# A hybrid decoder trunk: half of the conv norm's rounding copies by ScalarE, the second half of the output weights asked for later, and another figure for GpSimd's additions in the scheduler's table

## Chip, cores and metric

One core of a Trainium2 chip. The metric is the device time of one execution in microseconds; lower is better. The engines are TensorE (PE), VectorE (DVE), ScalarE (ACT), GpSimd (POOL) and SyncE (SP), which here issues all the transfers.

## What is computed

x is 1024 tokens by 1024 channels, float32. Layer 1 mixes tokens by a causal convolution, layer 2 by sliding-window attention; after each come a norm, a squared-ReLU MLP with a norm, and a gated per-layer embedding. The change is about the first mixer and the norm and product behind it:

```python
def conformer_conv(x, w_in, b_in, w_dw, b_dw, ln_g, ln_b, w_out, b_out):
    h = x @ w_in + b_in
    a, gate = jnp.split(h, 2, axis=-1)
    h = a * jax.nn.sigmoid(gate)
    h = lax.conv_general_dilated(
        h, w_dw[:, None, :], window_strides=(1,), padding=[(CONV_WIDTH - 1, 0)],
        dimension_numbers=("NWC", "WIO", "NWC"), feature_group_count=D_MODEL) + b_dw
    h = jax.nn.silu(layer_norm(h, ln_g, ln_b))
    return h @ w_out + b_out
...
    for i in range(DEPTH):
        y = conformer_conv(...) if i < N_A_LAYERS else swa_sink_attention(...)
        x = layer_norm(DEEPNORM_ALPHA * x + y, mix_ln_g[i], mix_ln_b[i])
        x = layer_norm(DEEPNORM_ALPHA * x + sq_relu_mlp(x, mlp_w_up[i], mlp_w_down[i]), mlp_ln_g[i], mlp_ln_b[i])
        x = x + (p[i] @ ple_w_proj[i]) * jax.nn.sigmoid(x @ ple_w_gate[i])
```

DEPTH is 2, D_MODEL 1024, CONV_WIDTH 31, and N_A_LAYERS 1.

## The kernel before

**Products in three parts.** TensorE works in a rounded float32 (fp32r). To keep float32's accuracy each operand is split into a rounded high part and the rest, xh and xl, wh and wl, and each product is three: xh with wh, xh with wl, xl with wh. A split is a rounding copy (xh from x) and a subtraction (xl = x - xh). The copy of a weight is ScalarE's, its subtraction VectorE's; a weight comes as raw from a DMA, in units of 128 x 1024.

**The scheduler.** The program is not issued as it is written. A Recorder notes every operation, schedule() (line 334) then orders them, and issue() emits them from line 485, which is why all rows of the trace have L485. schedule() is a list scheduler: it plays the program through with a duration for each operation from cost() (line 304), takes the operation that can start first and among those the one written first (later(by) adds to that rank, after(x) makes an operation depend on x in the plan), and hands out buffers by tag from a fixed number of slots (SLOTS: five t, four z, two raw, five wh and wl, four E and so on). The plan fixes each engine's order and which buffer each tile gets; on the chip the engines follow that order and wait for real data. Operations of the engine "either" go to VectorE or GpSimd, whichever the plan has free first: an addition in the norm and one in the embedding. The plan also knows that VectorE and GpSimd share something: an operation on one that reads two operands from SBUF is lengthened by what the other still holds (lines 346 to 357, and `held`). So one changed duration can move operations on all engines from there on.

**The conv stage** (to about 250 us). For each of eight channel blocks c, TensorE makes a and gate from x (most by a seven-product scheme with sums t, g). VectorE and ScalarE gate them, split the result (zz) and hand it over through DRAM (scr), from where it comes back in another layout (B). The 31 taps are products with band matrices E, which ScalarE and VectorE build from the weights z: a rounding copy into the upper half and a subtraction into the lower half. One channel block (OWN) is done without TensorE: ScalarE multiplies (z from B), GpSimd adds (cst), VectorE does the other half (g). The result goes by transposes (tr) into Z, tiles of tags X and A.

**The conv norm and the output product** (from about 250 us). conv_ln(t0) takes two token tiles of 128, t0 = 0, 2, 4, 6: statistics, one scaling on VectorE (X) and one on GpSimd (A), then for f = 0, 2, 4, 6 four transposes, two silu activations by ScalarE into a tile t, and the split of t: the rounding copy xh (512 columns) and the subtraction xl, both VectorE's. The output product has two halves of columns; each half's weights are four units of two channel blocks, and token tiles 0 to 3 (t0 = 0 and 2) are taken before tiles 4 to 7. Units 0 and 1 of the first half are asked for ahead of the norm, units 2 and 3 (called 713 and 718 in the order, their split parts 750, 751 and 754, 755) after the first silu.

Of the kernel before, what the change touches and what calls it, by code (L numbers as in the profile page):

```python
# [13 lines left out]
ALU = mybir.AluOpType  # L14
# [198 lines left out]
class Recorder:  # L213
# [90 lines left out]
    def cost(self, o, outs, allv):  # L304
        e, n = o.eng, o.name
        f = outs[0].n if outs and isinstance(outs[0], View) else 1024
        if e == "tensor":
            if n == "transpose":
                return 113.5
            return max(109.0, f * 0.4427 + 5.5 * (f < HT))  # L310
        if e == "sync":
            return 380.0
        if e == "scalar":
            t = 60.0 + f * 0.85
            if n == "activation":
                t += sum(c for k, c in (("bias", 90.0), ("scale", 130.0), ("accum_out", 110.0)) if isinstance(o.kw.get(k), View))
            return t
        if e == "gpsimd":
            if n == "tensor_tensor":
                return 460.0 if o.kw["op"] == ALU.pow else 90.0 + 2.2 * f  # L320
            return 160.0 + 1.17 * f
        psum = any(v.buf.space == "PSUM" for v in allv)
        if n == "tensor_scalar" and not psum:
            return 100.0 + f * 0.69
        if n == "bn_stats":
            return 69.0 + 1.042 * allv[-1].n
        if n == "reduce_max":
            return 70.0 + allv[-1].n * 1.042
        if n == "reciprocal":
            return 60.0 + 6.3 * f  # L330
        t = 120.0 if isinstance(o.kw.get("scalar"), View) else 70.0
        return t + f * 1.042
# [185 lines left out]
class Emit:  # L518
# [353 lines left out]
    def conv(self):  # L872

        nc, d, ws = self.nc, self.d, self.ws
# [330 lines left out]
        def conv_ln(t0):  # L1205

            zs = []
            for t in (t0, t0 + 1):
                z = [Z[t // 4, t % 4, q] for q in range(2)]
                rs = self.stats(z)  # L1210
                for q in range(2):
                    (nc.gpsimd if q else nc.vector).tensor_scalar(out=z[q], in0=z[q], scalar1=rs[:, 0:1], scalar2=rs[:, 1:2], op0=ALU.mult, op1=ALU.add)
                zs.append(z)
            for f in range(0, KB, 2):
                blk = [slice((f + j) % 4 * P, ((f + j) % 4 + 1) * P) for j in range(2)]
                ps = self.transpose4([z[f // 4][:, b] for b in blk for z in zs], SLACK)
                sv = self.sb("t")
                for j in range(2):
                    half = slice(2 * j * P, 2 * (j + 1) * P)
                    nc.scalar.activation(  # L1220
                        sv[:, half], ps[:, half], AF.Silu, bias=lb[:, f + j : f + j + 1], scale=lg[:, f + j : f + j + 1]
                    )
                    silu.append(nc.ops[-1])
                sl = (slice(None), slice(f % 4, f % 4 + 2), slice(t0 % 4 * P, (t0 % 4 + 2) * P))
                sv = sv.rearrange("p (a b) -> p a b", a=2)
                xh, xl = (x[sl] for x in self.xT[f // 4, t0 // 4])
                nc.vector.tensor_copy(xh, sv)
                nc.vector.tensor_tensor(out=xl, in0=sv, in1=xh.bitcast(F32), op=ALU.subtract)

        second = [self.load_xT(1, kb) for kb in range(KB)]  # L1230
# [14 lines left out]
        ins = (x for c in range(8) for x in conv_in(c))  # L1245
        outs = (x for c in range(8) for x in taps(c))
        alone = taps_alone()
        made = 0
        for n in range(32 + LAG):
            next(ins, None)  # L1250
            if n >= LAG:
                next(outs, None)
            made += OWN_RATE if n >= OWN_FROM else 0
            while made >= 1:
                next(alone, None)
                made -= 1
            if n == 32:
                idle = (x[:, k, :] for q in (1, 0) for x in self.xT_quarter((q, 1), F32) for k in range(4))
                fill = self.embed(0, (0, 1), idle, lambda *v: stores.append(v))
            for k in range(WOVEN[n - 32] if n >= 32 else 0):  # L1260
                next(fill)
# [24 lines left out]
        marks, silu = [], []  # L1286
        for t in range(0, NT, 2):
            conv_ln(t)
            if t == 0:
                with nc.after(silu[0]):  # L1290
                    ws.add(*[d["w_out"][0, u] for u in range(2, 4)])
                    ws.pump()
            marks.append(self.xT[1, t // 4][1].buf.last)
# [955 lines left out]
```

## Time and profile before

| | us |
|---|---|
| median of 3 runs (lowest, highest) | 2121.67 (2120.52, 2124.4) |
| the profiled execution | 2122.42 |
| its span | 2120.7 |
| PE busy in it | 2101.1 (99%) |
| DVE busy | 1721.8 (81%) |
| ACT busy | 1233.0 (58%) |
| POOL busy | 323.8 (15%) |

The granted TensorE clock is 1.00 over the stretches that the prediction reads. A row of the timeline gives the start in the span, the duration, the engine, the line, the operation, output<-inputs by the names of the program, the count, and in brackets how long the engine was idle before and what ended that. A row of the groups gives the count, the busy time and the mean duration in ns, then the idle time ahead of it. Since matmuls overlap, their durations are longer than the time from one to the next.

### The profile page before, as it was taken

What the parts mean: (1) busy time and instruction counts of PE and PEld (TensorE: products, weight loads), DVE (VectorE), ACT (ScalarE), POOL (GpSimd) and SP (SyncE); (2) the same over time, 40 slices, a digit from 0 to 9 for tenths busy, and PEclk for the clock granted to TensorE, in tenths of its full rate; (3) what the DMA queues carried; (4) which work ended last, traced back from release to release, by engine and by line L of the source; (5) the groups of instructions that cost most, each with busy time, mean ns of one, the idle gap of its engine ahead of it and who ended that gap; (6) DMA issues with size and microseconds to landing.
All of it is one profiled execution on the core that took longest, in us unless ns stands there. A gap on an engine that the chain in (4) does not pass through costs nothing.

```text
span 2120.7 us, 29661 instructions
## 1 busy us (share of the span) xinstructions
PE 2101.1 (99%) x9912; PEld 1738.4 (82%) x9912; DVE 1721.8 (81%) x2754; ACT 1233.0 (58%) x2335; POOL 323.8 (15%) x551
## 2 busy tenths in 40 slices
PE   9999999999999999999999999999999999999999
PEld 7888888888888888888878878888888888888887
DVE  8899799987777879876975878699787768788688
ACT  6767644766566533334656888466666663333373
POOL 0523114100000000002131656150000000000041
PEclk9999999999999999999999999999999999999999
DMA  6668855887787747564586112677877885575735
GB/s 228 190 201 284 290 188 173 296 269 246 260 268 262 259 163 243 185 201 152 174 296 230 36 66 80 219 247 253 277 271 257 272 305 174 181 252 163 246 111 202
DMA packets 216601, 459.56 MB, mean 217 GB/s; under 512 B 21888, under 2 KB 52864, under 8 KB 216448
## 3 DMA queue, kind: packets, MB, share of 16 engines
q1 hardware_dynamic: 216448, 457.67, 64.3%
q8 instruction: 78, 1.28, 0.2%
q14 instruction: 75, 0.61, 0.1%
HBM read 311.57 MB, written 146.01 MB: 216 GB/s over the span
## 4 chain that ended last, share of the span: by engine, by line
PE 75%; ACT 3%; DVE 3%; DMA 2%; issue 1%; POOL 1%; SPq 0%; DVEq 0%; POOLq 0%; ACTq 0%
PE ps L485 57%; PE tr L485 18%; ACT z L485 2%; DVE z L485 1%; DVE t L485 1%; DMA wh<-gate_t 1%; DMA t<-proj 0%; POOL sm L485 0%; DVE sm L485 0%; ACT t L485 0%; DMA raw<-in_w_q_dram 0%; ACT wh L485 0%; DMA hid<-zz 0%; DVE g L485 0%; ACT g L485 0%
## 5 line engine op out<-in xcount | busy, mean ns | idle before, releaser
L485 PE MATMUL ps<-xh 128*128 128x512 f32 x636 | 247.4, 389 | 0.0
L485 PE MATMUL ps<-xl,xh 128*128 128x512 f32 x636 | 247.4, 389 | 0.0
L485 PE MATMUL ps<-xh,xl 128*128 128x512 f32 x636 | 247.4, 389 | 0.0
L485 POOL TENSOR_SCALAR sm<-sm 128x1 f32<-128x1 f32 x72 | 26.3, 369 | 1358.2 <-DVE A L485 624.7
L485 PE MATMUL ps<-xl,wh 128*128 128x512 f32 x484 | 189.4, 392 | 0.0
L485 PE MATMUL ps<-xh,wh 128*128 128x512 f32 x484 | 188.0, 392 | 1.0 <-ACT t L485 0.8
L485 PE MATMUL ps<-xh,wl 128*128 128x512 f32 x484 | 188.7, 390 | 0.0
L485 ACT CAST wh<-raw 128x1024 fp32r<-128x1024 f32 (+2 forms) x134 | 119.4, 895 | 87.0 <-PE ps L485 58.8
L485 PE MATMUL ps<-wh,xh 128*128 128x512 f32 x412 | 162.8, 396 | 3.0 <-DMA wh<-gate_t 2.0
L485 PE MATMUL ps<-wh,xl 128*128 128x512 f32 x412 | 162.7, 396 | 0.0
L485 PE MATMUL ps<-wl,xh 128*128 128x512 f32 x412 | 162.4, 395 | 0.0
L485 ACT CAST xh<-wh 128x1024 fp32r<-128x1024 f32 x76 | 79.7, 1049 | 118.6 <-PE ps L485 82.2
L485 PEld LDWEIGHTS ps<-xl,xh 128*128 128x128 f32 x636 | 119.4, 188 | 24.9
L485 PEld LDWEIGHTS ps<-xh,xl 128*128 128x128 f32 x636 | 119.3, 188 | 24.8
L485 PEld LDWEIGHTS ps<-xh 128*128 128x128 f32 x636 | 119.4, 188 | 24.7
L485 DVE TENSOR_TENSOR wl<-raw,wh 128x1024 fp32r<-128x1024 f32 (+2 forms) x100 | 98.5, 986 | 46.8 <-ACT wh L485 46.7
L485 ACT CAST wh<-g 128x512 fp32r<-128x512 f32 x136 | 80.9, 619 | 86.5 <-PE ps L485 48.5
L485 DVE TENSOR_TENSOR wl<-g,wh 128x512 fp32r<-128x512 f32 x136 | 92.0, 701 | 36.6 <-ACT wh L485 36.3
L485 ACT ACTIVATE t<-t 128x512 f32<-128x512 f32 x144 | 91.1, 632 | 43.2 <-DVE t L485 41.4
L485 DVE TENSOR_TENSOR xl<-wh,xh 128x1024 fp32r<-128x1024 f32 x76 | 92.9, 1223 | 20.2 <-ACT xh L485 19.9
L485 PEld LDWEIGHTS ps<-xh,wh 128*128 128x128 f32 x484 | 90.7, 188 | 22.6 <-ACT t L485 1.8
L485 PEld LDWEIGHTS ps<-xh,wl 128*128 128x128 f32 x484 | 90.9, 188 | 18.7
(447 smaller groups left out, 5711.9 us busy)
## 6 DMA issues: line engine op xcount, KB each, us to landing
wh<-hid SPq DMA_DIRECT2D x78, 512.0 KB, 4.4
raw<-in_w_up_dram SPq DMA_DIRECT2D x68, 512.0 KB, 4.3
wl<-in_w_down_dram SPq DMA_DIRECT2D x58, 512.0 KB, 4.7
hid<-zz SPq DMA_DIRECT2D x96, 256.0 KB, 4.7
hid<-t SPq DMA_DIRECT2D x64, 256.0 KB, 4.7
z<-in_w_dw_dram SPq DMA_DIRECT2D x56, 288.0 KB, 4.3
raw<-hid SPq DMA_DIRECT2D x30, 512.0 KB, 3.6
hid<-z SPq DMA_DIRECT2D x36, 256.0 KB, 4.9
```

The lines of the kernel that those rows point to most:

```text
L485: getattr(getattr(nc, o.eng), o.name)(*a, **k)
```

## The change

```diff
@@ cost()
             if n == "tensor_tensor":
-                return 460.0 if o.kw["op"] == ALU.pow else 90.0 + 2.2 * f
+                return 460.0 if o.kw["op"] == ALU.pow else 120.0 + 2.3 * f
@@ conv_ln()
                 xh, xl = (x[sl] for x in self.xT[f // 4, t0 // 4])
-                nc.vector.tensor_copy(xh, sv)
+                (nc.scalar.copy if f % 4 else nc.vector.tensor_copy)(xh, sv)
                 nc.vector.tensor_tensor(out=xl, in0=sv, in1=xh.bitcast(F32), op=ALU.subtract)
@@ conv()
-        made = 0
+        made, seen, pace = 0, 0, []
         for n in range(32 + LAG):
             next(ins, None)
             if n >= LAG:
                 next(outs, None)
+            pace += [o for o in nc.ops[seen:] if o.eng == "tensor"][-1:]
+            seen = len(nc.ops)
@@ conv()
         for t in range(0, NT, 2):
             conv_ln(t)
-            if t == 0:
-                with nc.after(silu[0]):
+            if t == 2:
+                with nc.after(silu[9]):
                     ws.add(*[d["w_out"][0, u] for u in range(2, 4)])
                     ws.pump()
```

In the table, an addition of f columns on GpSimd now counts 120 + 2.3 f ns: 709 for 256 columns where it was 653, 1298 for 512 where it was 1216. In conv_ln the copies for f = 2 and f = 6 are ScalarE's, eight of sixteen. The output weights' units 2 and 3 are asked for after conv_ln(2), in the plan no earlier than its second activation. `pace` and `seen` are used nowhere else.

On SP's queue the two loads of units 2 and 3, which stood ahead of five loads of x, stand behind them. Of the additions that may go to either engine, three go from GpSimd to VectorE, all in the last norm and the last embedding. The counts of everything else are the same. In the attention stage the order is the same on all engines but for buffer numbers; in the conv stage, in the norm behind it, in the MLPs' stores and loads, and in the last norm rows have moved. Three places follow; the numbers in a name tell one tile from another, and differ between the two kernels for the same thing.

VectorE, conv stage, the build of the bands E (z: weights; wl, t, g, zz: pieces of the gating). Before, the subtraction for E_41 stands three rows above this piece, and the piece ends with that for E_42:

```order
L485 TENSOR_TENSOR wl_408_1042<-raw_387_887,wh_407_1039 128x1024
L485 TENSOR_TENSOR t_372_803<-t_372_803,ps_355_675 128x512
L485 TENSOR_TENSOR g_385_871<-g_385_871,ps_365_767 64x512
L485 TENSOR_TENSOR t_372_803<-t_372_803,t_351_644 128x512
L485 TENSOR_TENSOR g_398_965<-g_397_953,raw_387_887 128x512
L485 TENSOR_TENSOR zz_409_1047<-t_372_803,zz_409_1047 128x512
L485 TENSOR_TENSOR g_385_871<-g_385_871,ps_371_802 64x512
L485 TENSOR_TENSOR wl_415_1106<-g_398_965,wh_414_1103 128x512
L485 TENSOR_TENSOR wl_415_1106<-g_397_953,wh_414_1103 128x512
L485 TENSOR_TENSOR t_406_1036<-t_406_1036,ps_384_865 128x512
L485 COPY t_386_881<-tr_81_145 128x4x64
L485 TENSOR_TENSOR E_42_106<-z_393_922,E_42_106 64x9x64
```

Now:

```order
L485 TENSOR_TENSOR wl_400_979<-raw_375_811,wh_399_977 128x512
L485 TENSOR_TENSOR zz_389_890<-t_378_825,zz_389_890 128x512
L485 TENSOR_TENSOR E_41_105<-z_390_894,E_41_105 64x9x64
L485 TENSOR_TENSOR E_42_106<-z_393_922,E_42_106 64x9x64
L485 TENSOR_TENSOR wl_409_1042<-raw_387_887,wh_408_1038 128x1024
L485 TENSOR_TENSOR t_372_803<-t_372_803,ps_355_675 128x512
L485 TENSOR_TENSOR g_385_871<-g_385_871,ps_365_767 64x512
L485 TENSOR_TENSOR t_372_803<-t_372_803,t_351_644 128x512
```

E_42's subtraction stands directly behind E_41's, and what was ahead of it comes after.

ScalarE, conv stage, later: t_564 is the emptying of the PSUM tile ps_521 (now t_560), g the gate's halves, z the products of the block that is done without TensorE. Before:

```order
L485 ACTIVATE g_558_2143<-ps_538_2012,cst_302 64x256
L485 COPY E_391_905<-z_559_2147 128x9x64
L485 ACTIVATE g_558_2143<-ps_538_2012,cst_302 64x256
L485 ACTIVATE z_381_843<-B_445_1332,cst_302 128x256 x2
L485 COPY E_392_916<-z_572_2192 128x9x64
L485 ACTIVATE g_558_2143<-ps_548_2077,cst_302 64x256
L485 ACTIVATE t_564_2164<-ps_521_1903,cst_302 128x512
L485 ACTIVATE g_558_2143<-ps_548_2077,cst_302 64x256
```

Now:

```order
L485 ACTIVATE g_558_2135<-ps_540_2019,cst_302 64x256 x2
L485 COPY E_391_905<-z_565_2166 128x9x64
L485 ACTIVATE z_381_843<-B_445_1332,cst_302 128x256
L485 ACTIVATE g_558_2135<-ps_542_2028,cst_302 64x256 x2
L485 ACTIVATE z_381_843<-B_445_1332,cst_302 128x256 x2
L485 COPY E_392_916<-z_573_2196 128x9x64
L485 ACTIVATE t_560_2148<-ps_521_1901,cst_302 128x512
L485 ACTIVATE z_381_843<-B_445_1332,cst_302 128x128 x2
```

Both of g's rows from one PSUM tile come before the copy into E_392, and that t's row is right behind that copy; the row of g that stood between the two is gone from there.

The conv norm: VectorE's first rounding copies (xh<-t) and what stands around them (X: the scaling of a token tile, sm: statistics). Before:

```order
L485 TENSOR_SCALAR X_592_2289<-X_592_2289,sm_68_132 128x512
L485 TENSOR_SCALAR X_594_2295<-X_594_2295,sm_71_135 128x512
L485 BN_STATS sm_701_2999<-A_583_2263 128x6
L485 BN_STATS sm_734_3195<-X_615_2440 128x6
L485 COPY xh_241_305<-t_649_2673 128x2x256
L485 COPY xh_241_305<-t_650_2675 128x2x256
L485 TENSOR_TENSOR xl_242_306<-t_649_2673,xh_241_305 128x2x256
```

Now:

```order
L485 TENSOR_SCALAR X_592_2292<-X_592_2292,sm_68_132 128x512
L485 TENSOR_SCALAR X_595_2298<-X_595_2298,sm_71_135 128x512
L485 BN_STATS sm_701_3000<-A_584_2262 128x6
L485 COPY xh_241_305<-t_650_2680 128x2x256
L485 BN_AGGR sm_729_3168<-sm_701_3000 128x2
L485 BN_STATS sm_735_3198<-X_611_2422 128x6
L485 TENSOR_TENSOR xl_242_306<-t_650_2680,xh_241_305 128x2x256
L485 TENSOR_TENSOR xl_242_306<-t_651_2683,xh_241_305 128x2x256
```

The first copy stands behind one BN_STATS where it stood behind two; others come between the copies. ScalarE at the same place, with the rounding copies wh_750 and wh_754 of the output weights' units 2 and 3. Before:

```order
L485 ACTIVATE t_765_3320<-ps_763_3311,cst_302 128x256
L485 ACTIVATE t_769_3343<-tr_767_3333,cst_302 128x256 x2
L485 COPY A_759_3291<-A_587_2276 128x512
L485 COPY wh_750_3266<-raw_713_3069 128x1024
L485 COPY wh_754_3277<-raw_718_3098 128x1024
L485 ACTIVATE t_772_3352<-tr_768_3338,cst_302 128x256
```

Now:

```order
L485 COPY A_759_3290<-A_588_2277 128x512
L485 ACTIVATE t_779_3389<-tr_781_3398,cst_302 128x256 x2
L485 ACTIVATE t_775_3368<-tr_776_3370,cst_302 128x256
L485 ACTIVATE t_778_3382<-ps_777_3374,cst_302 128x256
L485 ACTIVATE t_775_3368<-tr_776_3370,cst_302 128x256
L485 ACTIVATE t_778_3382<-ps_777_3374,cst_302 128x256
L485 COPY wh_750_3264<-raw_713_3070 128x1024
L485 COPY xh_742_3222<-t_778_3382 128x2x256
L485 ACTIVATE t_784_3410<-tr_786_3424,cst_302 128x256
L485 COPY wh_754_3276<-raw_718_3100 128x1024
```

The two copies were behind the activations of conv_ln(2); now the first is behind six activations of conv_ln(4) (t_779, t_775, t_778), and an xh copy and another activation stand between the two.

## The prediction

> **What bounds the kernel now.** I read the page's first part, then the chain of waits, then busy time in stretches of the span, then every wait of TensorE (PE) from 50 to 345 us in the timeline, and last what the other engines did just before each of those waits.
>
> ```profile
> PE 2101.1 (99%) x9912; PEld 1738.4 (82%) x9912; DVE 1721.8 (81%) x2754; ACT 1233.0 (58%) x2335; POOL 323.8 (15%) x551
> ...
> 50.00:250.00 200.00, 195.47 (x1105) 168.66 (x1104) 174.44 (x275) 142.81 (x289) 64.98 (x89) 1.00 0.77 235
> 250.00:345.00 95.00, 93.21 (x463) 77.14 (x462) 88.42 (x163) 43.90 (x84) 22.29 (x34) 1.00 0.63 216
> 345.00:1000.00 655.00, 654.83 (x2918) 541.42 (x2917) 522.87 (x746) 350.88 (x542) 29.85 (x35) 1.00 0.69 232
> ```
>
> The columns of the stretches are from:to, length, then busy PE, weight loads, VectorE (DVE), ScalarE (ACT), GpSimd (POOL), the granted clock, the DMA share and GB/s. PE is busy 99% of the span at clock 1.00, so an edit to other engines pays only where PE waits. Over the MLP (345 to 1000) PE idles 0.17 us in 655: nothing there to win. In the conv stage (50 to 250) it idles 4.53, in the conv norm and the start of the output product (250 to 345) 1.79: together 6.3 us, and that is the change's field. These are the larger waits in it:
>
> ```profile
> 85.34 0.86 PE L485 MATMUL ps<-B,E 128*128 128x256 f32 x5 [0.66 <-DVE E L485]
> 94.95 0.50 PE L485 MATMUL ps<-xh,wh 128*128 128x512 f32 x1 [0.30 <-ACT t L485]
> 114.99 1.22 PE L485 MATMUL ps<-B,E 128*128 128x256 f32 x8 [0.84 <-DVE E L485]
> 154.70 1.07 PE L485 MATMUL ps<-B,E 128*128 128x256 f32 x7 [1.62 <-DMA B<-scr]
> 185.82 0.50 PE L485 MATMUL ps<-xh,wh 128*128 128x512 f32 x1 [0.55 <-ACT t L485]
> 186.16 0.39 PE L485 MATMUL ps<-xl,wh 128*128 128x512 f32 x1
> 186.39 0.39 PE L485 MATMUL ps<-xh,wl 128*128 128x512 f32 x1
> 266.94 0.55 PE L485 MATMUL tr<-ident,X 128*128 128x128 f32 x3 [0.43 <-DVE X L485]
> 268.45 0.50 PE L485 MATMUL ps<-wh,xh 128*128 128x512 f32 x1 [0.97 <-DVE xh L485]
> ```
>
> A matmul lasts 0.39 us, but the next starts 0.23 us behind it (186.16, 186.39): they overlap by 0.16. A wait breaks that overlap, so an idle time g costs g + 0.16. By this count the seven waits cost 0.82, 0.46, 1.00, 1.78, 0.71, 0.59 and 1.13.
>
> **The change part by part.** It does four things, and because every instruction of the program goes through the list scheduler, one changed duration reorders all that follows.
>
> *GpSimd's additions counted longer.* The scheduler's figure for 256 columns goes from 653 to 709 ns. What the trace shows:
>
> ```profile
> L485 POOL TENSOR_TENSOR cst<-cst,z 128x256 f32<-128x256 f32 x58 | 58.3, 1005 | 29.6 <-ACT z L485 23.0 <-ACT cst L485 2.5 <-DMA z<-in_w_dw_dram 1.4
> L485 DVE TENSOR_TENSOR E<-z,E 64x576 fp32r<-64x576 f32 x56 | 44.9, 807 | 10.8 <-ACT E L485 8.9 <-PE ps L485 1.7
> ```
>
> 58 additions lasted 1005 ns on average, so the new figure is nearer and still short. No instruction is added or removed; what comes of it is order. In the attention stage the order is the same as before on all engines but for buffer numbers, so the term is zero there; between 50 and 345 it is not. I take the waits one at a time.
>
> At 85.34 PE waits for the band E_42:
>
> ```profile
> 84.20 1.08 DVE L485 TENSOR_TENSOR E<-z,E 64x576 fp32r<-64x576 f32 x1
> ...
> 85.47 1.41 DVE L485 TENSOR_TENSOR E<-z,E 64x576 fp32r<-64x576 f32 x2
> ```
>
> That subtraction stood on VectorE thirteen rows behind E_41's; now it is directly behind it. Thirteen rows, most of 0.3 to 1.2 us, are some 8 us; the matmuls keep their place on PE. The wait goes whole: **-0.82** (bounds -0.82 and 0).
>
> The Trainium skill, "SBUF — State Buffer", section "Who interferes with whom", says that a VectorE instruction with two SBUF inputs and a GpSimd instruction that reads SBUF exclude each other: the second blocks for the whole of the first. By this rule the 1.08 us above, beside 0.70 each for the two bands at 85.47, holds a block of 0.4 us, and the moved band could meet another of up to 1.0; against some 8 us gained the term would stay -0.82 by rule and by rows alike. The rule speaks against the change in another place, among the rivals.
>
> At 94.95 and 185.82 PE waits for ScalarE to empty a PSUM tile into t:
>
> ```profile
> 93.71 0.60 ACT L485 CAST wh<-g 128x512 fp32r<-128x512 f32 x1
> 94.22 0.68 ACT L485 ACTIVATE t<-ps,cst 128x512 f32<-128x512 f32 x1
> 183.89 0.68 ACT L485 CAST E<-z 128x576 fp32r<-128x576 f32 x1 [1.10 <-DMA z<-in_w_dw_dram]
> 184.59 0.47 ACT L485 ACTIVATE g<-ps,cst 64x256 f32<-64x256 f32 x1
> 185.08 0.69 ACT L485 ACTIVATE t<-ps,cst 128x512 f32<-128x512 f32 x1
> ```
>
> Before the second, the order had a band copy and then one g ahead of t; now both g's come before the band copy and t stands right behind it. That takes one activation of 0.49 (184.59 to 185.08) out from between, against 0.55 of idle. For the first I only see that the rows ahead of t are other ones. A wait that is about one instruction long, and whose queue is rearranged, more likely goes than stays; I book both, **-0.46** and **-0.71**, with bounds 0 and the same again as a loss (+1.17 the two).
>
> At 154.70 PE waits for hand-over data that comes back from DRAM: ScalarE's rounding, GpSimd's addition, VectorE's subtraction and a store and a load hang behind each other. VectorE's part is moved up by one short step; the rest of the chain is as long as it was. Bounds 0 and -1.78; with one link of several moved I take half, **-0.89**. At 114.99 the same rows stand ahead of the band as before; only GpSimd's own order around it moves. Bounds 0 and -1.00, half: **-0.50**.
>
> *Half of the rounding copies go to ScalarE.*
>
> ```profile
> 265.15 1.74 DVE L485 TENSOR_SCALAR X<-X,sm 128x512 f32<-128x512 f32 x2
> 266.81 0.67 DVE L485 BATCH_NORM_STATS2 sm<-A 128x6 f32<-128x512 f32 x1
> 267.41 0.67 DVE L485 BATCH_NORM_STATS2 sm<-X 128x6 f32<-128x512 f32 x1
> 268.00 0.74 DVE L485 CAST xh<-t 128x512 fp32r<-128x512 f32 x2
> 268.66 1.28 DVE L485 TENSOR_TENSOR xl<-t,xh 128x512 fp32r<-128x512 f32 x2
> ...
> 274.10 2.04 ACT L485 CAST wh<-raw 128x1024 fp32r<-128x1024 f32 x2
> 284.50 0.56 ACT L485 ACTIVATE t<-tr,cst 128x256 f32<-128x256 f32 x1 [8.37 <-issue]
> ```
>
> Eight copies leave VectorE (0.33 each from start to start: 2.7 us) and cost ScalarE, by its own cast of that shape (a mean of 0.65 over four), 5.2 us. ScalarE idles 8.37 us in one piece ahead of 284.50, so the work is hidden; with that cover gone it would be the 5.2. On the path it shows once: the first xh copy now stands behind one BN_STATS instead of two, 0.60 us earlier, and PE waits 0.97 for it at 268.45. **-0.60** (bounds 0 and -1.13).
>
> ```profile
> L485 ACT CAST A<-A 128x512 fp32r<-128x512 f32 x4 | 2.3, 650 | 0.0
> ```
>
> *The weights' second half asked for later.* On SP's queue two loads go behind five loads of x:
>
> ```profile
> 264.62 0.92 SPq L485 DMA_DIRECT2D raw<-in_w_out_dram  x2
> 265.58 3.04 SPq L485 DMA_DIRECT2D E<-in_x_dram  x4
> ...
> 275.22 1.23 DVE L485 TENSOR_TENSOR wl<-raw,wh 128x1024 fp32r<-128x1024 f32 x1 [0.86 <-ACT wh L485]
> ...
> 280.84 0.39 PE L485 MATMUL ps<-wh,xh 128*128 128x512 f32 x1
> ...
> 269.94 1.48 ACT L485 ACTIVATE t<-tr,cst 128x256 f32<-128x256 f32 x3 [1.57 <-DVE xl L485]
> ...
> raw<-in_w_up_dram SPq DMA_DIRECT2D x68, 512.0 KB, 4.3
> ```
>
> Five loads of x at 0.76 are 3.8 us, so the two are issued by 269.3; weights of that size land 4.3 us after their issue (the last row, from the page's DMA part), so at some 273.6, ahead of the 274.10 at which ScalarE split them so far: zero for the loads. What counts is the split's new place, behind conv_ln(4)'s activations. Needed: unit 2's first product, by the order the 49th of the stage, started at 280.84. From 268.45 that is 12.4 us for 48 products at 0.23 (11.0) and 12 transposes, so 0.11 for each of these. With a start 0.6 earlier and 16 more transposes ahead (1.8) it is due at 282.0. Ready: from the first xh copy at 267.4 VectorE has ahead of wl_751 six copies (0.33), nine subtractions (0.60), four BN_STATS (0.60), two TENSOR_SCALARs (0.87) and four short ones (0.1), 11.9 us, plus its own 1.2: 280.5 if it never waits. Slack 1.5 us: zero in the sum, but thin, and a rival.
>
> *The end.* One of GpSimd's last additions goes to VectorE:
>
> ```profile
> 2107.96 2.66 DVE L485 TENSOR_TENSOR t<-t,t 128x512 f32<-128x512 f32 x2 [0.70 <-ACT t L485]
> ...
> 2111.57 0.69 DVE L485 TENSOR_TENSOR t<-t,t 128x512 f32<-128x512 f32 x1 [0.22 <-ACT t L485]
> ...
> 2108.79 1.28 POOL L485 TENSOR_TENSOR B<-B,t 128x512 f32<-128x512 f32 x1 [3.41 <-PE ps L485]
> ```
>
> Two products of 0.69 lasted 2.66 beside it. VectorE would be done sooner, but at 2111.57 it waits for ScalarE anyway: zero (bounds 0 and -0.4). The unused bookkeeping emits nothing.
>
> Sum: -0.82 - 0.46 - 0.71 - 0.89 - 0.50 - 0.60 = **-3.98**. The profiled execution took 2122.42 (span 2120.7), 0.75 above the median of 2121.67. So 2118.44 on its scale, and 2117.7 against the median.
>
> **Rivals.** *The waits move instead of going.* For it: the scheduler's 709 still stands beside 1005 measured, so the plan is off almost as before, and where VectorE and GpSimd overlap an instruction can double (2.66 for two of 0.69); what one PE wait loses another row gains. Against: E_42's move is far larger than such a block. Price: E_42's 0.82 alone stays; 2122.42 - 0.82 - 0.75 = 2120.9. By the Trainium skill's rule above (the same section) this is what reordering under an exclusive lock would do; whether the blocks move with the order no row of the profile before can say.
>
> *All of it goes.* The seven waits are 6.49, and of the 6.32 of idle between 50 and 345 their own 5.37 leave 0.95 of small ones: 7.4. For it: in the order PE's rows and those of its feeders are shifted in all these places. Against: the DRAM round trip at 154.70 has no shorter chain. 2122.42 - 7.4 - 0.75 = 2114.3.
>
> *Slower: the second half's split becomes the wait.* ScalarE works its queue in order; wh_750 and wh_754 now stand behind six activations (three in 1.48 at 269.94, so 2.9) and the second behind an xh copy, VectorE's wl behind those, and behind wl stand conv_ln(6)'s pieces, for which the products of the last four token tiles wait. If VectorE waits more than 1.5 us for ScalarE, PE stops at unit 2; then all eight copies (5.2), the activations (2.9) and the second split (1.2) can lie on the path: +9.3, with the conv stage's -3.38 kept and the norm's -0.60 lost: 2122.42 + 9.3 - 3.38 - 0.75 = 2127.6. For it: the slack is thin, and before the change the split was done at 276.4, 4 us ahead of need. Against: 8.37 us of ScalarE idle.
>
> *It doesn't do what it says:* the loads come only some 4 us later and meet nobody; that is in the sum as zero.
>
> **How the numbers follow.** What can be told from no change here is about 0.2%, 4.2 us: faster is below 2117.4, slower above 2125.9. The forecast gets 0.45, and its own range (2115.5 to 2120) straddles the bound: 0.22 faster, 0.23 no change. All goes: 0.20, faster. Waits move: 0.13, 0.10 no change and 0.03 slower (a moved wait may also grow, by the +1.17 and more). The late split: 0.22, 0.19 slower and 0.03 no change. That is 0.42 faster, 0.36 the same, 0.22 slower. The range goes from 2111 (all waits and some of the other small ones) to 2128 (just past the late split).
>
> **What would show it.** Right: no wait for E near 85; none for t near 94 and 185; the first product of the output stage within 0.5 us of its transposes; no PE wait at unit 2 (about 282); PE idle from 50 to 345 down from 6.3 to about 3. Wrong: PE waiting for wl or wh near 282 or for xh in the second half of the token tiles (the late split); new waits for E, g or B elsewhere in 50 to 250 with the sum unchanged (waits move); or a difference in the MLP or the attention stage, which nothing here foresees.

## The result: slower by 0.2%

The changed kernel takes 2126.64 us (median of 15 runs, 2123.78 to 2131.15), the kernel before 2122.64 (median of 15, 2119.56 to 2124.51): a ratio of 1.0022 with a 95% interval of 1.0015 to 1.0029, some 4 to 5 us. The forecast was 4 us the other way. The profiled execution has a span of 2126.2, 5.5 more than before; its time of 2127.88 is 1.2 above the median, so the 5.5 us taken apart below are somewhat more than the usual difference.

The page's first part and the busy time by stretches of the changed kernel (columns as before: length, busy PE, weight loads, VectorE, ScalarE, GpSimd, granted clock, DMA share, GB/s):

```profile
PE 2103.5 (99%) x9912; PEld 1742.5 (82%) x9912; DVE 1722.1 (81%) x2749; ACT 1235.5 (58%) x2343; POOL 322.1 (15%) x548
...
50.00:250.00 200.00, 193.41 (x1072) 166.84 (x1071) 172.04 (x273) 139.39 (x282) 62.16 (x89) 0.99 0.74 227
250.00:345.00 95.00, 92.56 (x476) 77.16 (x476) 84.61 (x149) 52.21 (x99) 28.76 (x31) 1.00 0.68 232
345.00:1000.00 655.00, 654.05 (x2909) 541.49 (x2908) 522.71 (x746) 347.46 (x533) 26.30 (x32) 1.00 0.68 232
```

Of the 5.5 us, 3.1 are more idle time of TensorE (22.7 against 19.6, span less busy) and 2.4 are more *busy* time with the same 9912 matmuls: they ran slower somewhere, and the clock of 0.99 in the first stretch says where to look. The idle time grew by 2.06 in the conv stage (6.59 against 4.53), by 0.65 in the norm and the product behind it, and by 0.78 in the stretch that begins at 345; over all other stretches it sums to 0.33 less. TensorE's larger waits in the changed kernel, from its timeline:

```profile
95.75 0.50 PE L485 MATMUL ps<-xh,wh 128*128 128x512 f32 x1 [0.97 <-ACT t L485]
116.90 0.62 PE L485 MATMUL ps<-B,E 128*128 128x256 f32 x3 [0.88 <-DVE E L485]
155.61 0.50 PE L485 MATMUL ps<-xh,wh 128*128 128x512 f32 x1 [0.18 <-ACT t L485]
187.89 0.79 PE L485 MATMUL ps<-xh,wh 128*128 128x512 f32 x1 [3.00 <-ACT t L485]
226.06 0.63 PE L485 MATMUL ps<-B,E 128*128 128x256 f32 x3 [0.74 <-DMA B<-scr]
272.38 0.50 PE L485 MATMUL ps<-wh,xh 128*128 128x512 f32 x1 [0.38 <-DVE xh L485]
295.95 0.44 PE L485 MATMUL tr<-ident,A 128*128 128x128 f32 x2 [1.54 <-POOL A L485]
383.09 0.66 PE L485 MATMUL ps<-ident,B 128*128 128x128 f32 x4 [0.72 <-POOL B L485]
2065.23 0.50 PE L485 MATMUL ps<-wh,xh 128*128 128x512 f32 x1 [1.13 <-DVE xl L485]
```

Against the list of before: the wait for E at 85 and the wait for the hand-over at 155 are gone, xh's fell from 0.97 to 0.38. But the wait for t that was 0.55 at 186 is 3.00, and three stand where none was: for GpSimd's A at 296, for GpSimd's B at 383, for VectorE's xl at 2065. Readings of the two largest led to the experiments: theory 1 puts the loss down to the first of them, theory 2 to the second.

**The wait at 188.** ScalarE just before it, and SP's queue, which issues the loads:

```profile
179.80 0.81 ACT L485 ACTIVATE g<-ps,cst 64x256 f32<-64x256 f32 x2
183.71 0.67 ACT L485 CAST E<-z 128x576 fp32r<-128x576 f32 x1 [3.10 <-DMA z<-in_w_dw_dram]
184.29 0.51 ACT L485 ACTIVATE z<-B,cst 128x256 f32<-128x256 f32 x1
184.82 0.83 ACT L485 ACTIVATE g<-ps,cst 64x256 f32<-64x256 f32 x2
185.67 0.91 ACT L485 ACTIVATE z<-B,cst 128x256 f32<-128x256 f32 x2
186.58 0.67 ACT L485 CAST E<-z 128x576 fp32r<-128x576 f32 x1
187.16 0.68 ACT L485 ACTIVATE t<-ps,cst 128x512 f32<-128x512 f32 x1
...
175.44 0.57 SPq L485 DMA_DIRECT2D bo<-in_b_out_dram  x1
176.50 1.02 SPq L485 DMA_DIRECT2D z<-in_w_dw_dram  x1
```

ScalarE stands for 3.10 us at the band copy E_391 for weights whose load, by the order of the loads, was issued at 176.50 and is there at 183.7, 7.2 us later; between it and t, which TensorE needs, stand six more instructions, another band copy among them. In the kernel before, SP had the corresponding piece in another order, and ScalarE made the band without a wait:

```profile
174.66 0.33 SPq L485 DMA_DIRECT2D z<-in_w_dw_dram  x1
175.26 0.38 SPq L485 DMA_DIRECT2D scr<-zz  x1
175.73 0.80 SPq L485 DMA_DIRECT2D bo<-in_b_out_dram  x1
...
180.95 0.66 ACT L485 CAST E<-z 128x576 fp32r<-128x576 f32 x1
```

There a load of band weights goes ahead of a hand-over's store and of bo; now it goes behind both.

**The wait at 296.** GpSimd scales the last token tile while VectorE adds the bias to the residual (six additions from 291.73 on):

```profile
265.40 0.77 POOL L485 TENSOR_SCALAR A<-A,sm 128x512 f32<-128x512 f32 x1
...
290.92 4.98 POOL L485 TENSOR_SCALAR A<-A,sm 128x512 f32<-128x512 f32 x1 [0.89 <-issue]
...
290.67 0.68 DVE L485 TENSOR_TENSOR E<-E,bo 128x512 f32<-128x512 f32 x1
291.27 0.54 DVE L485 TENSOR_SCALAR X<-X,sm 128x512 f32<-128x512 f32 x1
291.73 3.69 DVE L485 TENSOR_TENSOR E<-E,bo 128x512 f32<-128x512 f32 x6
```

The scaling took 4.98 us where the first of its kind took 0.77. It ends at 295.90, half a microsecond after the last of the additions, and TensorE starts at 295.95.

### The profile page after: what moved, and what is told of

The parts are those of the page before. It is cut to its first block, busy times and chain, and to the rows that moved or that the text cites. A ratio compares the mean times of both kernels' runs of the same rounds, so it can differ in the third digit from the quotient of the medians.

```text
span 2126.2 us, 29652 instructions
## 1 busy us (share of the span) xinstructions
PE 2103.5 (99%) x9912; PEld 1742.5 (82%) x9912; DVE 1722.1 (81%) x2749; ACT 1235.5 (58%) x2343; POOL 322.1 (15%) x548
## 5 line engine op out<-in xcount | busy, mean ns | idle before, releaser
L485 PE MATMUL ps<-xh,wh 128*128 128x512 f32 x496 | 193.9, 394 | 5.4 <-ACT t L485 4.5
L485 PE MATMUL ps<-xl,wh 128*128 128x512 f32 x496 | 195.1, 394 | 0.0
L485 PE MATMUL ps<-xh,wl 128*128 128x512 f32 x496 | 194.0, 391 | 0.0
L485 PE MATMUL ps<-wh,xh 128*128 128x512 f32 (+1 forms) x420 | 166.8, 397 | 2.7 <-DVE xl L485 1.1
L485 PE MATMUL ps<-wh,xl 128*128 128x512 f32 (+1 forms) x420 | 165.8, 396 | 0.0
L485 PE MATMUL ps<-wl,xh 128*128 128x512 f32 (+1 forms) x420 | 165.3, 394 | 0.0
```

The costliest lines, as they stand in the source:

```text
L485: getattr(getattr(nc, o.eng), o.name)(*a, **k)
```

## The experiments

Each kernel ran five rounds beside the kernel before on the same chip; a ratio is given against that.

### The parts one by one

```diff
 cost_only:     +  120.0 + 2.3 * f
 act_only:      +  (nc.scalar.copy if f % 4 else nc.vector.tensor_copy)(xh, sv)
 late_only:     +  if t == 2:  with nc.after(silu[9]):
 act_and_late:  both of the last two
```

The figure alone:

> The kernel before with only GpSimd's additions counted as 120 + 2.3 f. Theory 1 (the new figure reorders the conv stage for the worse: behind a rounding of band weights that arrive late from DRAM, ScalarE empties t late and TensorE waits 3.0 us at 188): about +3 to +4 us against before, with that wait of some 3 us for t near 188 in the profile, and the norm behind it much as before. Theory 2 (the loss is in the norm and output product: GpSimd's scaling of a token tile beside six additions of VectorE, 1.5 us at 296): within 1 us of before, and no wait over 1 us near 188.

The other two parts together:

> The kernel before with the other two parts, ScalarE's copies and the later request, and the old figure for GpSimd. Theory 1: within 1 us of before, the conv stage's waits as before (0.66 at 85, 1.62 at 155). Theory 2: +2 to +4 us, with a TensorE wait of 1 us or more for GpSimd's A in the output product (285 to 300).

The copies alone:

> The kernel before with only the eight rounding copies on ScalarE. Theory 1: within 1 us of before. Theory 2 splits here: if the copies themselves set off the late scaling by GpSimd, +1 to +2 us and a wait for A; if not, within 1 us.

The later request alone:

> The kernel before with only the later request for the weights' units 2 and 3. Theory 1: within 1 us of before. Theory 2 as in the last run: +1 to +2 us if the request sets it off, else within 1 us. The rival of the prediction (the split too late for unit 2) would show as a TensorE wait for wl or wh near 281.

| | median | before beside it | ratio (95%) |
|---|---|---|---|
| cost_only | 2123.83 | 2122.04 | 1.0005 (0.9997 to 1.0014) |
| act_and_late | 2124.74 | 2122.04 | 1.0012 (1.0003 to 1.0021) |
| act_only | 2123.03 | 2122.04 | 1.0005 (0.9996 to 1.0013) |
| late_only | 2123.47 | 2122.04 | 1.0006 (0.9997 to 1.0015) |

By the times neither theory wins. Each of the three parts alone is within what can be told; act_and_late alone is clear of 1, by 2.7 us of the medians, which lies in theory 2's range, and cost_only is 1.8 above, less than theory 1 asked. The two halves, 1.0005 and 1.0012, make up most of 1.0022. The profiles say more. TensorE's waits, two of cost_only, one of late_only, one of act_and_late, and GpSimd's last scaling in late_only:

```profile
186.77 0.80 PE L485 MATMUL ps<-xh,wh 128*128 128x512 f32 x1 [3.11 <-ACT t L485]
...
381.73 0.44 PE L485 MATMUL tr<-ident,B 128*128 128x128 f32 x2 [2.36 <-POOL B L485]
```

```profile
292.72 0.55 PE L485 MATMUL tr<-ident,A 128*128 128x128 f32 x3 [0.89 <-POOL A L485]
...
287.68 4.98 POOL L485 TENSOR_SCALAR A<-A,sm 128x512 f32<-128x512 f32 x1 [4.53 <-ACT wh L485]
```

```profile
293.28 0.33 PE L485 MATMUL tr<-ident,A 128*128 128x128 f32 x1 [1.78 <-POOL A L485]
```

The wait at 188 comes with the figure, and so do those for B at 383 and, at the end, for xl. GpSimd's scaling of 4.98 us comes with the later request, without the figure; the copies alone do not bring it. Both theories name a true part. Theory 1's estimate of +3 to +4 for the figure was too high; one likely reason is that the figure also takes waits away (those for E at 85 and for the hand-over at 155 are not in cost_only's profile either), but what each is worth was not measured.

### What holds TensorE at 188, and at 296

The experiments from here on keep the scheduler's plan and change only the named instructions in it: after schedule() a table moves an instruction on its engine, and everything else stays in its order. after_again is the change itself issued that way, the base for the rest.

```diff
 t_first (ScalarE):
+ACTIVATE t_560<-ps_521
 COPY E_391<-z_565
 ...
 COPY E_392<-z_573
-ACTIVATE t_560<-ps_521
 last_scaling:
-GpSimd   TENSOR_SCALAR A<-A,sm      (the last of eight)
+VectorE  TENSOR_SCALAR A<-A,sm      (ahead of X_616 and the six additions)
 three_moves: both, and
-GpSimd   TENSOR_TENSOR B<-z,g  x2   (the norm behind the product, last token tiles)
+VectorE  TENSOR_TENSOR B<-z,g  x2
```

> The changed kernel itself, issued in the same order on all engines, as the base for the three that follow. Both theories: +4 to +5 us against before, as measured; TensorE waits of about 3.0 us near 188 (t), 1.5 near 296 (A) and 0.7 near 383 (B).

> The changed kernel with one instruction moved: on ScalarE the emptying of the PSUM tile into t (t_560) stands ahead of the rounding of the band weights E_391, for which ScalarE waited 3.10 us. Theory 1 (the order on ScalarE makes the wait): TensorE's wait near 188 falls from 3.0 to under 0.7, and the kernel comes down by 2 to 3 us. Rival (the band weights' loads set the pace there, the DMA engines being over nine tenths busy): TensorE stops within 15 us behind for E or B instead, and the kernel stays within 1 us.

> The changed kernel with one instruction on another engine: the last scaling of the conv norm (A, token tile 7) goes from GpSimd, where it lasted 4.98 us beside six additions of VectorE, to VectorE ahead of five of them. Theory (those additions hold it up, and TensorE waits for it): the wait of 1.5 us near 296 goes, 1.2 to 1.7 us faster than the changed kernel. Rival (TensorE waits there for the statistics or for VectorE anyway): a wait of 1 us or more for X or xh takes its place.

> Both moves, and two additions of the first norm behind the product (B, token tile 6 and the first half of 7) on VectorE instead of GpSimd, where three in a row lasted 5.16 us. If the three waits add up: 4 to 5.5 us below the changed kernel, so level with before (within 1 us). If what they release waits elsewhere: 1 to 3 us below it.

| | median | before beside it | ratio (95%) |
|---|---|---|---|
| after_again | 2125.14 | 2121.30 | 1.0020 (1.0011 to 1.0029) |
| t_first | 2125.40 | 2121.30 | 1.0018 (1.0009 to 1.0028) |
| last_scaling | 2123.19 | 2121.30 | 1.0010 (1.0001 to 1.0019) |
| three_moves | 2122.66 | 2121.30 | 1.0010 (1.0001 to 1.0018) |

t_first is the clearest miss. The wait for t goes, the time stays. TensorE's waits in it:

```profile
186.23 0.44 PE L534 MATMUL tr<-ident,g 128*128 128x128 f32 x2 [1.74 <-DVE g L534]
...
200.62 0.44 PE L534 MATMUL tr<-ident,g 128*128 128x128 f32 x2 [0.94 <-ACT t L534]
...
224.49 0.39 PE L534 MATMUL ps<-B,E 128*128 128x256 f32 x1 [1.54 <-DMA B<-scr]
```

The 3.0 us came back in three places (of the last, 0.60 was in after_again too): t's row on ScalarE was where the delay was seen, not what made it. ScalarE's row of t, now in front of E_391, shows why little could be won:

```profile
182.94 0.69 ACT L534 ACTIVATE t<-ps,cst 128x512 f32<-128x512 f32 x1 [3.01 <-PE ps L534]
```

In its new place t waited 3.01 us for TensorE's own products, and E_391 and the rows of g behind it came no earlier than with the late load. So the move doesn't tell by itself what makes the load late. The rival holds in its time, and not in what it named: within 15 us TensorE stopped for g and t, and for B only 38 us behind.

last_scaling is 1.95 us below the base by the medians, a little more than the 1.2 to 1.7 expected, and the wait at 296 is gone; the intervals of the two ratios overlap, so the times alone do not show the gain. In its profiled execution (2126.12, 2.9 above its median) TensorE waited longer for B a little later instead, 2.23 against 0.34 in after_again. three_moves, with two additions more on VectorE and t's move as well, cut that to 0.22:

```profile
380.24 0.33 PE L534 MATMUL ps<-ident,B 128*128 128x128 f32 x1 [2.23 <-POOL B L534]
```

By the medians that last step brought 0.5 us, less than can be told. In all, three_moves is 2.5 us below after_again, in the range named for the case that what the moves release waits elsewhere.

### What makes the weights late

```diff
 loads_later (SP; GpSimd's scalings of bo moved behind with them):
-DMA raw<-in_w_proj   (ahead of the store to scr)
-DMA bo<-in_b_out     (ahead of z)
-DMA bo<-in_b_out     (ahead of two loads of X)
+DMA raw<-in_w_proj   (ahead of the loads B<-scr)
+DMA bo<-in_b_out x2  (behind the loads B<-scr)
 later_and_two:        and the scaling and the two additions of three_moves
 figure_mended:        the figure alone, the loads, the two additions
 without_the_request:  the figure and the copies, the loads, the two additions
```

> The changed kernel with three loads moved on SP's queue behind the band weights that came late: the two of bo (256 KB each, and GpSimd's two scalings of bo, for which it waited 2.98 us) and one of the embedding's weights (512 KB). No other engine's order differs. If the band weights' loads set the pace near 188 because the DMA engines are full: ScalarE's wait for z falls from 3.1 to under 1.5 us, TensorE's waits near 188 to 225 from 3.9 to under 2, and the kernel comes down by 1 to 3 us. If the slots of z (a load can only be issued when a band is built) set it: the wait stays above 2.5 us and the time within 1 us.

> The same with the last scaling and the two additions of the first norm on VectorE as well. If the parts add up: 3 to 5 us below the changed kernel, level with before or up to 1 us faster.

> The kernel before with the new figure alone, the three loads moved as above and the two additions of the first norm on VectorE. With the figure alone the profile had TensorE waits of 3.1 us near 187 and 2.4 near 382; if both go: 2 to 4 us faster than before, the first version that beats it. If the waits only move: within 1.5 us of before.

> The kernel before with the new figure and ScalarE's copies but the weights' second half asked for as before, the three loads moved and the two additions of the first norm on VectorE. If the later request is what runs GpSimd's last scaling into the six additions: no TensorE wait for A near 291, and 1.5 to 3.5 us faster than before. If the copies alone bring it: the wait of 1.5 us is back, and within 1.5 us of before.

| | median | before beside it | ratio (95%) |
|---|---|---|---|
| loads_later | 2122.76 | 2121.78 | 1.0006 (0.9997 to 1.0015) |
| later_and_two | 2120.69 | 2121.78 | 0.9994 (0.9985 to 1.0003) |
| figure_mended | 2119.35 | 2121.78 | 0.9994 (0.9986 to 1.0003) |
| without_the_request | 2122.46 | 2122.72 | 0.9999 (0.9990 to 1.0008) |

loads_later changes three loads' places and nothing that computes, but for bo's own scalings. SP, then ScalarE, in it:

```profile
175.83 0.33 SPq L534 DMA_DIRECT2D z<-in_w_dw_dram  x1
...
179.55 0.42 SPq L534 DMA_DIRECT2D raw<-in_w_proj_dram  x1
...
183.38 0.50 SPq L534 DMA_DIRECT2D bo<-in_b_out_dram  x1
...
179.93 0.66 ACT L534 CAST E<-z 128x576 fp32r<-128x576 f32 x1
...
183.41 0.68 ACT L534 ACTIVATE t<-ps,cst 128x512 f32<-128x512 f32 x1
```

The same load (by its place in the order) is there after 4.1 us at most (175.83 to 179.93) instead of 7.2, ScalarE doesn't wait, t comes at 183.41 instead of 187.16. TensorE from 170 to 190, in the changed kernel and then in loads_later:

```profile
170.00:190.00 20.00, 17.00 (x92) 14.60 (x91) 16.55 (x23) 14.28 (x31) 12.12 (x20) 0.95 0.92 290
```

```profile
170.00:190.00 20.00, 20.00 (x119) 17.56 (x118) 19.67 (x29) 15.68 (x33) 12.20 (x19) 1.00 0.88 282
```

From 17.0 busy and a clock of 0.95 to 20.0 and 1.00: the wait is gone and nothing takes its place there. By the medians 2.9 us of the 3.8 to before came back (3.84 with after_again, 0.98 here), by moving bytes that TensorE did not need yet (GpSimd had waited 2.98 us for bo, and its scalings of bo moved along). That shows the cause of this wait: other loads issued just ahead of the band weights, at a DMA share of 0.92 over these 20 us. In the three other versions with the loads moved it is 0.41 or none; in the four with the loads as they were and t in its place it is 1.97 to 3.11. Which of the three loads matters most was not tried.

figure_mended and later_and_two have medians 2.4 and 1.1 us below the kernel before; their intervals include 1, so neither is shown to beat it. figure_mended's forecast of 2 to 4 us was for both large waits gone: the one near 187 went, but TensorE still waits 1.71 for B at 378.62, now for VectorE. without_the_request fell short of its forecast too (TensorE waits 0.96 for A), and shows that the later request is not needed for GpSimd's long scaling:

```profile
284.94 4.98 POOL L534 TENSOR_SCALAR A<-A,sm 128x512 f32<-128x512 f32 x1 [0.89 <-issue]
```

The request alone brings the scaling of 4.98 us, and so do the figure and the copies together; the figure alone and the copies alone do not, nor does figure_mended, which differs from without_the_request by the copies alone. It is a matter of the order that comes out, not of one part.

## Why the prediction was wrong

The frame held in the main: from 420 to 1000 TensorE has no idle time in the changed kernel, the change's field was the conv stage and the norms, and the price of a wait is its length and a little more, except where the clock falls behind it (last section). The step that failed most is the term of -0.71 for the wait at 185.82: it went by the instructions ahead of t, and the load of the band weights ahead of them made that wait 3.00. Going by its own steps:

- **The wait at 85 (-0.82): right.** There is no wait there in the changed kernel.
- **154.70 (-0.89, half of 1.78): right, and undersized.** 1.62 became 0.18, for something else. Part of that may be luck: in act_only and late_only, which have the old figure, the same wait was 0.81 and 0.51, so the 1.62 of the one profiled execution is not a firm size.
- **114.99 (-0.50): wrong by its size.** 0.84 became 0.88: the wait stayed.
- **94.95 (-0.46): wrong.** 0.30 became 0.97. "The rows ahead of t are other ones" was no reason for a gain. The size is loose: in versions that keep this piece of the order it was 0.27 (later_and_two) to 0.82 (loads_later).
- **185.82 (-0.71): wrong, and the largest single error.** The step read "that takes one activation of 0.49 out from between". In the row that it quoted stood what mattered: ScalarE, at the band copy E<-z (by the order E_392), was itself idle for 1.10 "<-DMA z<-in_w_dw_dram". What stood ahead of t waited for loads, not only for its turn. In the changed kernel it was the load of the copy before, E_391, that came late by its place on SP's queue; E_391 held all that stood behind it on ScalarE, and 0.55 became 3.00. The bound of +1.17 for this wait and the one at 95 was far too narrow. That rows of the conv stage had moved was in the text of the change; no term asked whether SP's loads were among them, and what stood ahead of z there.
- **The xh copies (-0.60): right in size, wrong in its cause.** 0.97 became 0.38 in the changed kernel. With the copies on ScalarE alone (first) it stayed, with the figure alone (second) it fell:

```profile
268.19 0.50 PE L485 MATMUL ps<-wh,xh 128*128 128x512 f32 x1 [0.96 <-DVE xh L485]
```

```profile
271.23 0.50 PE L485 MATMUL ps<-wh,xh 128*128 128x512 f32 x1 [0.37 <-DVE xh L485]
```

- **The second half's split (zero; the slower rival if late): right as to the term.** In the changed kernel TensorE has no wait of note between 272.4 and 295.9, and in that stretch, at 284.83 and 286.75, VectorE makes wl of units 2 and 3. The rival looked at the right stage and the wrong queue: what came late was GpSimd's scaling, 1.54 us, for which the prediction had no row at all, though GpSimd feeds half of each token tile there.
- **The end (zero): wrong, unexplained.** TensorE waits 1.13 for xl at 2065, and 1.12 to 1.16 in every version with the new figure, in none without it. That this follows from the additions that went to VectorE is likely and wasn't tried.
- **The rivals.** "The waits move instead of going" was the mechanism that decided, at a chance of 0.13, and with a time of 2120.9, which let a wait come back at most at its old length. t_first shows waits that do so; the change itself shows that a load moved on a full queue can make a wait several times the one it replaces. The range reached up to 2128 only for the late split, which did not happen: that the measured time lies inside it is luck.

The rule of the Trainium skill that was weighed, on VectorE and GpSimd excluding each other ("SBUF — State Buffer", section "Who interferes with whom"), agrees with the trace as far as it goes: 4.98 us for a scaling of 0.77. It tells of one instruction that blocks another; here the scaling lasted through seven. The prediction applied it to the band subtractions of the conv stage, where the waits it could cause were covered, and not to the norm, where its price was 1.5 us of TensorE's time.

## What to carry to other kernels

Before booking a moved instruction as a gain, read what the instructions ahead of it on its engine wait for: if one of them waits for a DMA, the gain is decided on the DMA's queue, so list what was issued ahead of that load before and after the change. A cost table that sets an order by list scheduling changes waits everywhere it reaches, and the sum of many small ones of both signs is not told by the few that the old profile shows; a forecast from those alone should be wide on the slower side too. Loads without a deadline (a bias used 100 us later) belong behind those that a full DMA queue makes late.

## What the runs showed of the hardware that was not expected

**A wait can be charged twice, and where it falls decides.** After the 3.00 us at 187.89 the next matmuls start 0.57 to 0.43 us apart instead of 0.23, for some 3.5 us. The kept traces have the granted clock at 0.50 for 3.41 us at a time; last_scaling's falls twice, at 186.52 and 381.08, 57 such lengths apart. So I cut the span into stretches of that length, counted from such a fall. The changed kernel's wait of 3.00, last_scaling's of 1.97 (to 185.85) and cost_only's of 2.36 (to 381.73), each with the stretch that follows:

```profile
184.51:187.92 3.41, 0.41 (x3) 0.03 (x1) 2.86 (x4) 3.36 (x8) 2.42 (x6) 1.00 1.07 376
187.92:191.33 3.41, 3.41 (x10) 2.84 (x11) 2.98 (x7) 1.27 (x4) 1.77 (x2) 0.50 0.98 345
```

```profile
183.11:186.52 3.41, 1.44 (x9) 0.91 (x8) 2.95 (x4) 3.38 (x9) 2.95 (x6) 1.00 1.02 355
186.52:189.93 3.41, 3.41 (x11) 2.74 (x10) 3.24 (x9) 0.63 (x2) 1.25 (x2) 0.50 1.06 385
```

```profile
377.54:380.95 3.41, 1.83 (x9) 1.18 (x7) 2.08 (x5) 2.64 (x4) 2.08 (x3) 1.00 0.95 293
380.95:384.36 3.41, 2.63 (x16) 2.27 (x17) 3.38 (x3) 3.41 (x8) 3.41 (x3) 1.00 0.60 226
```

The clock fell behind stretches in which TensorE was busy for 0.41 and 1.44 us, and not behind one with 1.83: cost_only's wait was longer than last_scaling's, but lay across the end of a stretch. In all fourteen traces it fell behind the five stretches with 1.44 us or less (1.18 the other one of last_scaling, 0.59 in after_again, 0.68 in cost_only) and behind none with 1.67 or more, as in act_and_late at 291.54, counted from where that trace's clock is first full. A clock of 0.50 for 3.41 us costs 1.7 us, most of the 2.4 us by which TensorE's busy time grew. The Trainium skill, "TensorE: Matmul & The Clock Gate", section "Part 1: The HAM clock gate", puts the throttling at an idle window of about 3.4 us; here the length agrees, but a stretch that was idle for 1.97 of its 3.41 us was enough.

Not every execution is charged. Nine of the changed kernel's 15 have a mean clock below 1.000, with a median of 2127.8; the other six have 2124.5, some 1.9 above the kernel before. In loads_later all 11 have 1.000, so the 2.9 us that it brought back hold the clock's part too. So by a rough estimate half of the slowdown is the clock (rough, because some executions of the kernel before have such a mean clock too and are no longer).

**A GpSimd scaling can be held through a whole run of VectorE's additions.** The scaling that started at 290.92 was held through one scaling and six additions of VectorE back to back, and VectorE's lost nothing (3.69 us for six, 0.62 each). It is not always so. In act_only the same scaling, again started 0.25 us into an addition with one scaling and five additions to come, got its turn, and one addition was the longer for it:

```profile
286.85 1.38 POOL L485 TENSOR_SCALAR A<-A,sm 128x512 f32<-128x512 f32 x1 [0.36 <-issue]
...
287.66 1.10 DVE L485 TENSOR_TENSOR E<-E,bo 128x512 f32<-128x512 f32 x1
```

What decides between the two was not tried. Such a run of additions is a bad neighbour for the one GpSimd instruction that TensorE waits for.
